# One 512-column matmul for the high weights in place of two of 256, with a split accumulator

## The chip, the cores and the metric

The kernel runs on one core of a Trainium2 chip. The metric is the device time of one execution in microseconds (us); less is better. The engines are called PE (TensorE, matmuls; PEld is its weight load), DVE (VectorE), ACT (ScalarE), POOL (GpSimd) and SP (which here only starts transfers). TensorE's granted clock is 0.992 of full speed as a mean over the profiled span.

## The reference

A trunk of two decoder layers over 256 positions, model width 2048. Every sub-layer computes h = RMSNorm(x) * (1 + scale) + shift, and then x += gate * f(h), where shift, scale and gate are linear in SiLU(c) (one vector c of 2048, weights `ada_w`).

- Layer 0: one input projection (`ab_w_in`), latent attention and a gated DeltaNet on its columns, one output projection (`ab_w_out`).
- Layer 1: gated linear attention ("GLA", `gla_w_in`, `gla_w_out`).
- After each: a SwiGLU feed-forward network ("FFN"), `(silu(h @ w1) * (h @ w3)) @ w2`, with 5632 inner columns. The two are called FFN 0 and FFN 1.
- At the end one RMSNorm.

All inputs and the output are float32.

## The kernel before

**Matmuls in parts.** A weight tile arrives as float32 (`raw`). ACT rounds it to float32r (`hi`, L255) and DVE subtracts (`lo = raw - hi`, L256, which the profile shows as L195). Activations are split in the same way into two halves of one tile, `hl[:, 0]` (high) and `hl[:, 1]` (low), 256 tokens each. `mm3` (L263) then makes a product of three matmuls: hi x high, hi x low and lo x high, each with a stationary weight tile of 128 x 128, 256 moving columns, and the same [128, 256] PSUM accumulator. Below, such three matmuls are a *triple*: one k-tile (128 rows of the weights) of one block (128 output columns).

**Streaming.** `stream_T` (L269) computes 512 output columns at a time: a *group* of four blocks with one PSUM bank each (`acc`, a pool of four banks in all, L141). A weight load (`wload`, 512 rows x 512 columns, 1 MB) serves 16 triples: four blocks of four k-tiles. There are four `hi` and four `lo` buffers of two k-tiles each, so the load for the second wload ahead can be split only when PE lets go of a buffer. A group's block is emptied after its last k-tile by `evac`, and the next group's block of the same number needs that bank.

**Who empties what.** In the FFN `evac1` (L1267: ACT, SiLU), `evac3` (L1272: DVE product, then the split for the next product), and `x_add` (L472: DVE, x += gate * acc) after `w2`. `x_add` also follows the two output projections; the first of these is cut into three parts over k (k-tiles 0 to 7, 8 to 11, 12 to 15), so each of its 16 blocks is added three times. The GLA projections copy their accumulators out (L1330, L1346).

**Order.** A scheduler places each engine's instructions in advance; each engine then runs its own list in order. In between, DVE makes `ada` sums (L202, `ada<-araw,sc,ada`: 128 x 512 multiply-adds of `ada_w`) at a rate tied to the weight loads, until they are all done, in layer 1's GLA; FFN 1 has none. In FFN 0 these keep their program order.

Of the kernel before, what the change touches and what calls it, by code (L numbers as in the profile page):

```python
# [26 lines left out]


def _constants():
# [20 lines left out]
    # out[m] = sum_k lhsT[k, m] x[k]  # L50
# [32 lines left out]
def weave(main, back, n_back=1, rest=True):  # L83
    """Emit `main`, with `n_back` steps of `back` after each of its steps; then the rest of `back`."""
    due = 0.0
    for _ in main:
        due += n_back
        while due >= 1 - 1e-9:
            due -= 1
            if next(back, StopIteration) is StopIteration:  # L90
                due = -1e9
    if rest:
        drain(back)


def braid(*gens):
    """The generators' steps in turn."""
# [34 lines left out]
class Trunk:  # L132
# [74 lines left out]
    def lnexp(s):  # L207
        """Load the table set that has both logarithm and exponential."""
        s.tc.keep_in_program_order(s.nc.scalar.preload_act_table_set("natural_log_exp_and_others"))

    def tick(s, n):
        """n steps of the background stream."""
# [10 lines left out]
    def split(s, hl, x):  # L223
        """hl [128, 2, n] float32r: the high and the low part of x [128, n], which sum to x."""
# [3 lines left out]
    def rstd(s, out, ss, n, eps=EPS):  # L228
        """out = (ss / n + eps) ** -0.5, from logarithm and exponential with a Newton step."""
# [17 lines left out]
    def wload(s, src, k0, nk, c0, ncol, tick=False):  # L247
        """Per k-tile, the high and low parts of src's columns, [128, ncol] each."""
# [14 lines left out]
    def mm3(s, ps, w, hl, start, stop):  # L263
        """ps += w^T h: w (hi, lo) stationary, hl [128, 2, T] moving."""
# [3 lines left out]

    def stream_T(s, src, k0, hs, c0, ncol, evac, nk=None, prepare=None):  # L269
        """Blocks of (h @ src[k0.., c0:c0+ncol])^T; evac(block, psum [128, T])."""  # L270
# [3 lines left out]
        for t in range(0, nk, 4):  # L274
# [6 lines left out]
            for b in range(nb):  # L281
                for q in range(n):
                    w = tuple(x[:, b * 128:(b + 1) * 128] for x in ws[q])
                    s.mm3(ps[b][:, :T], w, hs[t + q], t + q == 0, t + q == nk - 1)
                if t + n == nk:
                    evac(b, ps[b][:, :T])
                yield

    def stream_few(s, src, k0, hs, c0, ncol, evac):
        """As stream_T, two blocks to a bank; evac(pair of blocks, psum [128, 2 T])."""  # L290
# [15 lines left out]
    def stream_narrow(s, pieces, k0, hs, out, start, stop):  # L306
        """At most four k-tiles of 80 columns: those of `pieces` [(src, c0, n)], then zeros; out psum [80, T]."""
# [18 lines left out]
    def ada_all(s, jobs, ahead=None, wide=False):  # L326
        """silu(c) @ ada_w[l, m] + ada_b for each job (l, m, cols, pe), `cols` being groups of four column tiles
        or [(first, number)], four at most; on the tensor engine or on the vector engine; the loads run ahead."""
# [32 lines left out]
    def ada_ends(s):  # L361
        """What is due of the ends of units."""
# [6 lines left out]
    def ada_flush(s):  # L369
        """All ends of the units that are done."""  # L370
# [48 lines left out]
    def ada_rows(s):  # L419
        """The sums over the partitions of the units in s.fin, in rows; ada_end is to follow."""  # L420
# [11 lines left out]
    def ada_end(s, a, us, sel):  # L432
        """Rows, 32 to a unit (or the one unit), to columns; with bias, and scale 1 + s times the norm's."""
# [38 lines left out]
    def x_add(s, l, m, k, ps):  # L472
        s.stt(s.x[:, k], ps, s.gate(l, m, k), s.x[:, k], ALU.mult, ALU.add)

    def x_square(s, k):
        """The square of x's k-tile, into the sum over them; of the last ones straight in the product with ones."""
# [34 lines left out]
    def setup(s):  # L511
# [36 lines left out]
        # 1 / rms of the tokens, then along the free axis  # L548
# [45 lines left out]
    def rope_tables(s):  # L594
        """cos and signed sin of positions * inv_freq, [128, T]; exact reduction for any int32 position."""
# [12 lines left out]
        n = s.d((128, 2, T))      # n1, n0  # L608
        r = s.d((128, 2, T))      # remainder, parts
        w = s.d((128, 2, T))  # L610
        # ang = n1 2^22 + n0 2^12 + a2
# [7 lines left out]
        # k = round((n1 b22 + n0 b12 + a2) / 2 pi)  # L619
# [6 lines left out]
        # coarse parts, on a grid of 2^-11, are exact  # L626
# [12 lines left out]
        # cos x = sin(x + pi/2), wrapped  # L639
# [9 lines left out]
    def in_proj(s):  # L649
# [24 lines left out]
        for c, nk in enumerate(chunks):  # L674
# [7 lines left out]
            for name, g, c0 in order:  # L682
# [30 lines left out]
                def evac1(b, ps):  # L713
                    f = P[name, 2 * g + b // 2][:, b % 2]
                    s.tt(f, ps, f, ALU.add)
# [19 lines left out]
    def conv(s, which, blk, out):  # L735
        """out = silu(causal depthwise convolution of block blk)."""
# [9 lines left out]
    def gdn(s):  # L746
# [37 lines left out]
        # natural layout: logarithms of the squared norms, decay and beta  # L784
# [8 lines left out]
        lnss = s.pers((128, 2, 2, 8), name="lnss")      # tile, (k, q), head  # L793
# [19 lines left out]
        bg = s.sv((128, 2, 16))       # ln beta, g  # L813
# [42 lines left out]
    def gdn_local(s, half):  # L856
        """Per head: the decayed products of keys and queries, and the natural layouts."""
# [4 lines left out]
        # L^T of the half's heads and chunks, with room to read it in steps of a block row and a block  # L862
        s.lt[half] = s.drp.tile([8, 8 * 2064], F32, name=s.nm("lt"))
        for hh in range(4 * half, 4 * half + 4):
# [30 lines left out]
            nt = s.d((128, 4, 128))       # beta v (both chunks), k for the state, k for w  # L895
# [7 lines left out]
    def gdn_blocks(s, half):  # L903
        """(I + L)^-1 of the blocks of 16 on the diagonal, and its transpose, by substitution, a block a partition;
        then as [128, (T, R), unit, 16], rows on partitions."""
# [8 lines left out]
        for _ in range(W0):       # steps of the others, while the blocks are on their way  # L914
# [18 lines left out]
    def gdn_merge(s, half):  # L933
        """R = (I + L)^-T from its blocks of 16. T = R^T and R are kept as their blocks of 32, [128, unit, 32],
# [700 lines left out]
```

## Time and profile before

| | |
|---|---|
| Median of 3 runs | 2667.74 us (2664.41 to 2672.6) |
| Profiled execution, span from first to last instruction | 2669.5 us |
| PE busy | 2635.0 us, 99% |
| PEld busy | 2448.4 us, 92% |
| DVE busy | 1752.1 us, 66% |
| ACT busy | 1158.9 us, 43% |
| DMA moved | 622.73 MB, 233 GB/s |

No time of the profiled execution is listed apart from its span; the span lies within the range of the timed runs, 1.8 us above their median. Busy time of PE counts pipelined matmuls that overlap, so the pace of matmuls is read from the distance of their starts, not from their durations.

### The profile page before, as it was taken

The page shows a single profiled execution, that of the slowest core. Times are in us where ns is not written, and L with a number is a line of the kernel's source. Part 1 is how long each engine was busy: PE and PEld are TensorE (multiplying, and loading weights), DVE is VectorE, ACT ScalarE, POOL GpSimd, SP SyncE. Part 2 cuts the span into 40 slices and gives each one's busy share as a digit, 9 for nine tenths or more (in the row PEclk, how much of TensorE's full clock was granted, in tenths as well). Part 3 has the DMA queues.
Part 4 walks back from the last instruction along what each step waited for, and adds up shares of the span by engine and source line. Part 5 has one row for each costly group of instructions (what it writes and reads, how often), then busy time and mean ns, then how long its engine had stood idle before and what let it go on. Part 6 is the DMA issues. An engine that isn't in the chain of part 4 may idle for free.

```text
span 2669.5 us, 49809 instructions
## 1 busy us (share of the span) xinstructions
PE 2635.0 (99%) x20850; PEld 2448.4 (92%) x20850; DVE 1752.1 (66%) x2566; ACT 1158.9 (43%) x1705; POOL 108.2 (4%) x166
## 2 busy tenths in 40 slices
PE   8999999999999999999999999999999999999998
PEld 5778886788999999999999998999999999999998
DVE  3655763678888878878889687775554544544544
ACT  4324574534433344333335444564444344333334
POOL 0000004002000000000002000002000000000001
PEclk9999999999999999999999999999999999999999
DMA  9886654787898889888896655545455555555553
GB/s 332 294 273 219 211 196 157 246 281 242 298 337 304 309 302 323 299 306 315 301 321 223 219 185 199 190 155 187 160 179 189 177 187 182 181 189 176 188 180 120
DMA packets 324111, 622.73 MB, mean 233 GB/s; under 512 B 20192, under 2 KB 31085, under 8 KB 323887
## 3 DMA queue, kind: packets, MB, share of 16 engines
q1 hardware_dynamic: 319998, 606.76, 66.6%
q0 software_dynamic: 3696, 12.72, 1.4%
q8 instruction: 163, 2.67, 0.4%
q14 instruction: 62, 0.50, 0.1%
q10 hardware_dynamic: 192, 0.08, 0.0%
HBM read 616.09 MB, written 3.41 MB: 232 GB/s over the span
## 4 chain that ended last, share of the span: by engine, by line
PE 97%; DMA 1%; DVE 1%; ACT 0%; issue 0%; SPq 0%; DVEq 0%; ACTq 0%
PE acc L192 87%; PE sm L192 6%; PE pa L192 4%; DMA araw<-in_ada_w 1%; DMA d<-in_ada_w 0%; ACT hi L255 0%; DVE lo L195 0%; DMA d<-in_x 0%; ACT d L205 0%; DVE tmp L195 0%; PE acc L1503 0%; DVE tmp L202 0%; PE acc L1218 0%; PE acc L893 0%; PE acc L894 0%
## 5 line engine op out<-in xcount | busy, mean ns | idle before, releaser
L192 PE MATMUL acc<-d,hi 128*128 128x256 f32 x12000 | 2193.7, 285 | 10.7 <-ACT d L205 10.4
L192 PEld LDWEIGHTS acc<-d,hi 128*128 128x128 f32 x12000 | 1876.2, 192 | 82.5 <-issue 35.7
L192 PE MATMUL acc<-d,lo 128*128 128x256 f32 x6000 | 1696.2, 284 | 0.0
L195 DVE TENSOR_TENSOR lo<-raw,hi 128x1024 fp32r<-128x1024 f32 (+2 forms) x801 | 946.5, 1204 | 615.8 <-ACT hi L255 592.3
L255 ACT CAST hi<-raw 128x1024 fp32r<-128x1024 f32 x776 | 781.7, 1045 | 1076.2 <-PE acc L192 932.0
L192 PEld LDWEIGHTS acc<-d,lo 128*128 128x128 f32 x6000 | 1150.2, 192 | 15.7 <-issue 13.8
L202 DVE SCALAR_TENSOR_TENSOR ada<-araw,sc,ada 128x512 f32<-128x512 f32 x480 | 362.7, 757 | 5.3
L202 DVE SCALAR_TENSOR_TENSOR x<-acc,mod,x 128x256 f32<-128x256 f32 x192 | 89.6, 480 | 61.9 <-PE acc L192 61.9
L195 DVE TENSOR_TENSOR d<-acc,d 128x256 f32<-128x256 f32 (+1 forms) x168 | 80.4, 486 | 71.9 <-PE acc L192 70.6
L192 PE MATMUL pa<-araw,sc 128*32 128x512 f32 x480 | 119.3, 611 | 5.4 <-DMA araw<-in_ada_w 5.3
L192 PE MATMUL acc<-hi,d 128*128 128x512 f32 (+1 forms) x320 | 93.4, 373 | 0.0
L225 ACT CAST d<-d 128x256 fp32r<-128x256 f32 x128 | 47.7, 404 | 49.7 <-DVE d L195 49.7
L192 PEld LDWEIGHTS acc<-hi,d 128*128 128x128 f32 x320 | 57.8, 189 | 10.6 <-ACT tmp L1203 0.8
L195 DVE TENSOR_TENSOR d<-d,d 128x256 fp32r<-128x256 f32 (+1 forms) x155 | 60.9, 421 | 8.9 <-ACT d L205 5.2
L205 ACT ACTIVATE d<-acc 128x256 f32<-128x256 f32 x96 | 36.7, 383 | 56.7 <-PE acc L192 56.7
L192 PE MATMUL acc<-lo,d 128*128 128x512 f32 (+1 forms) x160 | 59.9, 374 | 0.0
L195 POOL TENSOR_TENSOR ss<-ss,tmp 128x256 f32<-128x256 f32 x44 | 52.8, 1199 | 79.2 <-ACT tmp L205 77.5
L195 DVE TENSOR_TENSOR tmp<-d,tmp 128x512 f32<-128x512 f32 x64 | 43.7, 689 | 2.3 <-ACT tmp L205 1.9
L481 POOL COPY ss<-tmp 128x256 f32<-128x256 f32 x3 | 1.3, 421 | 964.3 <-ACT tmp L205 964.3
L205 ACT ACTIVATE d<-tmp,mod 128x256 fp32r<-128x256 f32 x64 | 28.6, 501 | 26.9 <-DVE tmp L202 14.2
L192 PEld LDWEIGHTS pa<-araw,sc 128*32 128x32 f32 x480 | 17.0, 107 | 24.7 <-DMA araw<-in_ada_w 8.2
L205 ACT ACT_TABLE_LOAD x28 | 35.9, 1283 | 3.5 <-DVE d L1350 1.4
(214 smaller groups left out, 1083.2 us busy)
## 6 DMA issues: line engine op xcount, KB each, us to landing
raw<-in_ffn_w SPq DMA_DIRECT2D x264, 1024.0 KB, 5.2
araw<-in_ada_w SPq DMA_DIRECT2D x347, 512.0 KB, 6.0
raw<-in_gla_w_in SPq DMA_DIRECT2D x48, 1024.0 KB, 5.1
raw<-in_ab_w_in SPq DMA_DIRECT2D x30, 1024.0 KB, 6.0
raw<-in_ab_w_out SPq DMA_DIRECT2D x16, 1024.0 KB, 6.9
raw<-in_gla_w_out SPq DMA_DIRECT2D x16, 1024.0 KB, 5.0
araw<-in_ada_w POOLq DMA_DIRECT2D x21, 512.0 KB, 4.2
raw<-in_ab_w_in SPq DMA_DIRECT2D x20, 512.0 KB, 5.9
```

Source lines behind the costliest of these rows:

```text
L192: s.nc.tensor.matmul(out, lhsT=lhsT, rhs=rhs, start=start, stop=stop)
L195: (eng or s.nc.vector).tensor_tensor(out=out, in0=a, in1=b, op=op)
L202: return s.nc.vector.scalar_tensor_tensor(out=out, in0=a, scalar=sc, in1=b, op0=op0, op1=op1)
L205: s.nc.scalar.activation(out, a, f, **kw)
L225: s.nc.scalar.copy(hl[:, 0], x)
L255: s.nc.scalar.copy(hi[:, :n, :ncol], raw[:, a:a + n, :ncol])
L481: s.nc.gpsimd.tensor_copy(s.ss, q)
```

## The change

The high weights multiply both halves of the activations in one matmul of 512 columns, whose output fills the whole bank: hi x high in the left 256 columns, hi x low in the right 256. The product lo x high goes to the left half. Per k-tile there are two matmuls where there were three, with the same 768 moving columns. After a block's first k-tile, lo stands ahead of hi. Whoever empties a bank adds its halves: `join` copies the right half with ACT and adds the left with DVE; `x_add` and `evac1` of the input projection make two DVE instructions of one. The other users of `mm3` keep it.

```diff
+    def mmw(s, ps, w, hl, first, last):
+        both = hl.rearrange("p a t -> p (a t)")
+        if first:
+            s.mm(ps, w[0], both, True, False)
+            s.mm(ps[:, :T], w[1], hl[:, 0], False, False)
+        else:
+            s.mm(ps[:, :T], w[1], hl[:, 0], False, False)
+            s.mm(ps, w[0], both, False, last)
+
+    def join(s, out, ps):
+        s.nc.scalar.copy(out, ps[:, T:])
+        s.tt(out, ps[:, :T], out, ALU.add)
...
-                    s.mm3(ps[b][:, :T], w, hs[t + q], t + q == 0, t + q == nk - 1)
+                    s.mmw(ps[b], w, hs[t + q], t + q == 0, t + q == nk - 1)
                 if t + n == nk:
-                    evac(b, ps[b][:, :T])
+                    evac(b, ps[b])
...
     def x_add(s, l, m, k, ps):
-        s.stt(s.x[:, k], ps, s.gate(l, m, k), s.x[:, k], ALU.mult, ALU.add)
+        for a in range(2):
+            s.stt(s.x[:, k], ps[:, a * T:(a + 1) * T], s.gate(l, m, k), s.x[:, k], ALU.mult, ALU.add)
...
                 def evac1(b, ps):
                     f = P[name, 2 * g + b // 2][:, b % 2]
-                    s.tt(f, ps, f, ALU.add)
+                    for a in range(2):
+                        s.tt(f, ps[:, a * T:(a + 1) * T], f, ALU.add)
...
-                    s.act(sl[b // 2][:, b % 2], ps, AF.Silu)
+                    a = sl[b // 2][:, b % 2]
+                    s.join(a, ps)
+                    s.act(a, a, AF.Silu)
...
                     t = sl[b // 2][:, b % 2]
-                    s.tt(t, ps, t, ALU.mult)
+                    u = s.tmp((128, T))
+                    s.join(u, ps)
+                    s.tt(t, u, t, ALU.mult)
...
-                    if nme == "q":
-                        s.act(dst[key][:, b % 2], ps, AF.Copy, scale=1.0 / 16.0)
-                    else:
-                        nc.vector.tensor_copy(dst[key][:, b % 2], ps)
+                    o = dst[key][:, b % 2]
+                    s.join(o, ps)
+                    if nme == "q":
+                        s.act(o, o, AF.Copy, scale=1.0 / 16.0)
...
-                (nc.scalar.copy if b % 2 else nc.vector.tensor_copy)(s.gr[key][:, b % 2], ps)
+                s.join(s.gr[key][:, b % 2], ps)
```

The scheduler makes new lists from this. First PE, at the end of one `w2` group of FFN 0 and the start of the next (in the kernel before, the end of the group of acc1557 to acc1560, a block's four k-tiles in a row; `hi1569` holds k-tiles 0 and 1 of a wload, `hi1572` k-tiles 2 and 3):

```order
L192 MATMUL acc1558_9289<-d1415_8134,hi1569_9357 128x256 x2
L192 MATMUL acc1558_9289<-d1415_8134,lo1570_9358 128x256
L192 MATMUL acc1558_9289<-d1416_8150,hi1569_9357 128x256 x2
L192 MATMUL acc1558_9289<-d1416_8150,lo1570_9358 128x256
L192 MATMUL acc1558_9289<-d1417_8166,hi1572_9365 128x256 x2
L192 MATMUL acc1558_9289<-d1417_8166,lo1573_9366 128x256
L192 MATMUL acc1558_9289<-d1418_8182,hi1572_9365 128x256 x2
L192 MATMUL acc1558_9289<-d1418_8182,lo1573_9366 128x256
L192 MATMUL acc1559_9290<-d1415_8134,hi1569_9357 128x256 x2
```

The same engine in the changed kernel, the very end of the group acc1573 to acc1576 (`hi1594` holds the last two of its 12 k-tiles) and the first rows of the next group, whose block 0 is acc1597:

```order
L192 MATMUL acc1573_8368<-d1500_7921,hi1594_8475 128x512
L192 MATMUL acc1574_8369<-d1498_7906,lo1595_8476 128x256
L192 MATMUL acc1574_8369<-d1498_7906,hi1594_8475 128x512
L192 MATMUL acc1574_8369<-d1500_7921,lo1595_8476 128x256
L192 MATMUL acc1574_8369<-d1500_7921,hi1594_8475 128x512
L192 MATMUL acc1575_8370<-d1498_7906,lo1595_8476 128x256
L192 MATMUL acc1575_8370<-d1498_7906,hi1594_8475 128x512
L192 MATMUL acc1575_8370<-d1500_7921,lo1595_8476 128x256
L192 MATMUL acc1575_8370<-d1500_7921,hi1594_8475 128x512
L192 MATMUL acc1576_8371<-d1498_7906,lo1595_8476 128x256
...
L192 MATMUL acc1576_8371<-d1500_7921,hi1594_8475 128x512
L192 MATMUL acc1597_8523<-d1349_6998,hi1602_8529 128x512
```

Two matmuls stand for three, and the blocks now take turns every two k-tiles: block 0 (acc1573) ends only three pairs of k-tiles before the group does, and the next group's block 0 follows at once.

Next DVE, which empties such a group in FFN 0. In the kernel before (group acc1557 to acc1560):

```order
L202 SCALAR_TENSOR_TENSOR x19_117<-acc1557_9288,mod16_114,x19_117 128x256
L202 SCALAR_TENSOR_TENSOR ada1567_9304<-araw1571_9361,sc11_104,ada1567_9304 128x512
L202 SCALAR_TENSOR_TENSOR x19_117<-acc1558_9289,mod16_114,x19_117 128x256
L202 SCALAR_TENSOR_TENSOR x19_117<-acc1559_9290,mod16_114,x19_117 128x256
L202 SCALAR_TENSOR_TENSOR ada1567_9304<-araw1574_9369,sc11_104,ada1567_9304 128x512
L202 SCALAR_TENSOR_TENSOR x19_117<-acc1560_9291,mod16_114,x19_117 128x256
L195 TENSOR_TENSOR lo1594_9560<-raw1592_9557,hi1593_9559 128x1024
```

In the changed kernel (group acc1573 to acc1576):

```order
L202 SCALAR_TENSOR_TENSOR x19_117<-acc1573_8368,mod16_114,x19_117 128x256
L195 TENSOR_TENSOR lo1610_8580<-raw1608_8577,hi1609_8579 128x1024
L202 SCALAR_TENSOR_TENSOR x19_117<-acc1574_8369,mod16_114,x19_117 128x256
L202 SCALAR_TENSOR_TENSOR x19_117<-acc1575_8370,mod16_114,x19_117 128x256
L202 SCALAR_TENSOR_TENSOR ada1583_8384<-araw1590_8433,sc11_104,ada1583_8384 128x512
L202 SCALAR_TENSOR_TENSOR x19_117<-acc1573_8368,mod16_114,x19_117 128x256
L202 SCALAR_TENSOR_TENSOR x19_117<-acc1576_8371,mod16_114,x19_117 128x256
L195 TENSOR_TENSOR lo1612_8584<-raw1608_8577,hi1611_8583 128x1024
L202 SCALAR_TENSOR_TENSOR x19_117<-acc1574_8369,mod16_114,x19_117 128x256
L202 SCALAR_TENSOR_TENSOR x19_117<-acc1575_8370,mod16_114,x19_117 128x256
L202 SCALAR_TENSOR_TENSOR ada1583_8384<-araw1590_8433,sc11_104,ada1583_8384 128x512
L202 SCALAR_TENSOR_TENSOR x19_117<-acc1576_8371,mod16_114,x19_117 128x256
```

A block's bank was free after one instruction; now the second half of block 0 is read after four others. In FFN 1, where no `ada` sums are left, only one `lo` stands between the two halves of block 0:

```order
L202 SCALAR_TENSOR_TENSOR x19_117<-acc3672_21052,mod16_114,x19_117 128x256
L195 TENSOR_TENSOR lo3702_21239<-raw3700_21236,hi3701_21238 128x1024
L202 SCALAR_TENSOR_TENSOR x19_117<-acc3672_21052,mod16_114,x19_117 128x256
L202 SCALAR_TENSOR_TENSOR x19_117<-acc3673_21053,mod16_114,x19_117 128x256
L202 SCALAR_TENSOR_TENSOR x19_117<-acc3674_21054,mod16_114,x19_117 128x256
```

The first `x` row and the third are the two halves of one block; before, there was one row for it.

## Rows read from the trace of the kernel before

**Rows 1.** The page: span, busy time of engines, and the chain that ended last.
```profile
span 2669.5 us, 49809 instructions
...
PE 2635.0 (99%) x20850; PEld 2448.4 (92%) x20850; DVE 1752.1 (66%) x2566; ACT 1158.9 (43%) x1705; POOL 108.2 (4%) x166
...
PE 97%; DMA 1%; DVE 1%; ACT 0%; issue 0%; SPq 0%; DVEq 0%; ACTq 0%
```

**Rows 2.** Timeline of FFN 1: start, length (us), engine, line, operation, tiles, count.
```profile
2000.24 0.40 PE L192 MATMUL acc<-d,hi 128*128 128x256 f32 x2
2000.37 0.19 PEld L192 LDWEIGHTS acc<-d,lo 128*128 128x128 f32 x1
2000.48 0.28 PE L192 MATMUL acc<-d,lo 128*128 128x256 f32 x1
2000.48 0.31 PEld L192 LDWEIGHTS acc<-d,hi 128*128 128x128 f32 x2
2000.60 0.40 PE L192 MATMUL acc<-d,hi 128*128 128x256 f32 x2
```

**Rows 3.** Timeline of PE in GLA's values, matmuls of 512 columns.
```profile
1639.95 0.61 PE L192 MATMUL acc<-hi,d 128*128 128x512 f32 x2
1640.40 0.39 PE L192 MATMUL acc<-lo,d 128*128 128x512 f32 x1
1640.63 0.61 PE L192 MATMUL acc<-hi,d 128*128 128x512 f32 x2
```

**Rows 4.** Lines by form, PE: count | busy us, mean ns | idle before, releasers.
```profile
L192 PE MATMUL acc<-d,hi 128*128 128x256 f32 x11936 | 2182.5, 285 | 10.7 <-ACT d L205 10.4 <-DVE d L195 0.2
L192 PE MATMUL acc<-d,lo 128*128 128x256 f32 x5968 | 1687.3, 284 | 0.0
```

**Rows 5.** Windows: stretch, length, busy us of PE, PEld, DVE, ACT, POOL, clock, DMA share, GB/s.
```profile
600.00:700.00 100.00, 96.02 (x730) 87.87 (x730) 84.01 (x139) 46.26 (x74) 15.61 (x12) 0.97 0.72 243
...
1000.00:1100.00 100.00, 100.00 (x825) 98.06 (x824) 81.75 (x114) 38.71 (x47) 0.00 (x0) 1.00 0.89 311
...
2100.00:2200.00 100.00, 100.00 (x836) 100.00 (x835) 48.05 (x54) 37.66 (x43) 0.00 (x0) 1.00 0.56 184
```

**Rows 6.** Lines by form, DVE, 700 to 1400 us (FFN 0).
```profile
L195 DVE TENSOR_TENSOR lo<-raw,hi 128x1024 fp32r<-128x1024 f32 x234 | 282.3, 1221 | 110.4 <-ACT hi L255 110.3
L202 DVE SCALAR_TENSOR_TENSOR ada<-araw,sc,ada 128x512 f32<-128x512 f32 x338 | 252.0, 748 | 4.3
L202 DVE SCALAR_TENSOR_TENSOR x<-acc,mod,x 128x256 f32<-128x256 f32 x48 | 22.5, 480 | 4.4 <-PE acc L192 4.4
L195 DVE TENSOR_TENSOR d<-acc,d 128x256 f32<-128x256 f32 x43 | 17.9, 421 | 3.8 <-PE acc L192 3.8
...
L199 DVE TENSOR_SCALAR ada<-araw,sc 128x512 f32<-128x512 f32 x23 | 11.0, 480 | 1.8 <-DMA araw<-in_ada_w 1.8
```

**Rows 7.** Timeline of DVE in FFN 0 (paces of its operations).
```profile
1016.27 0.42 DVE L195 TENSOR_TENSOR d<-acc,d 128x256 f32<-128x256 f32 x1
1016.60 0.42 DVE L195 TENSOR_TENSOR d<-d,d 128x256 fp32r<-128x256 f32 x1
1016.94 0.75 DVE L202 SCALAR_TENSOR_TENSOR ada<-araw,sc,ada 128x512 f32<-128x512 f32 x1
1017.60 0.42 DVE L195 TENSOR_TENSOR d<-acc,d 128x256 f32<-128x256 f32 x1
...
1044.74 2.32 DVE L202 SCALAR_TENSOR_TENSOR ada<-araw,sc,ada 128x512 f32<-128x512 f32 x3
1047.56 2.36 DVE L195 TENSOR_TENSOR lo<-raw,hi 128x1024 fp32r<-128x1024 f32 x2 [0.51 <-ACT hi L255]
```

**Rows 8.** Timeline of DVE in FFN 1, end of a w2 group.
```profile
2303.57 0.48 DVE L202 SCALAR_TENSOR_TENSOR x<-acc,mod,x 128x256 f32<-128x256 f32 x1 [0.96 <-PE acc L192]
2303.97 2.35 DVE L195 TENSOR_TENSOR lo<-raw,hi 128x1024 fp32r<-128x1024 f32 x2
2309.56 2.36 DVE L195 TENSOR_TENSOR lo<-raw,hi 128x1024 fp32r<-128x1024 f32 x2 [3.25 <-ACT hi L255]
```

**Rows 9.** Windows of 30 us at the end of layer 0's output projection, columns as in rows 5.
```profile
590.00:620.00 30.00, 30.00 (x204) 22.07 (x201) 21.25 (x37) 10.37 (x16) 0.00 (x0) 1.00 0.88 299
620.00:650.00 30.00, 30.00 (x250) 29.10 (x248) 28.91 (x46) 14.71 (x26) 15.61 (x12) 1.00 0.79 259
```

**Rows 10.** The chain in order of time, its last long piece: start, us, what.
```profile
1891.75 763.14 PE acc L192 x6336
```

## The prediction, made before the result was known

> **What bounds the kernel now.** I read the page first. PE is busy 99% of the span, its weight loads 92%, DVE 66%, and the chain that ended last is 97% PE [rows 1]. So time is won by what makes PE's list shorter, and lost by what lets PE wait. Busy time of PE doesn't say how fast it goes, since a matmul's row of 0.28 us overlaps the next; the timeline does. In FFN 1 the first hi matmul of a triple starts at 2000.24 us and the next triple's at 2000.60: 0.360 us for three matmuls of 256 columns, 0.120 each [rows 2]. 256 columns at 2.4 GHz (the granted clock in FFN 1 is 1.00 of it [rows 5]) are 106.7 ns, so each matmul costs 13.3 ns beside its columns. The kernel has matmuls of 512 columns too, in GLA's values: a round of three takes from 1639.95 to 1640.63, 0.680 us, so 226.7 ns each [rows 3]. 512 columns are 213.3 ns; the rest is 13.3 ns again. So there is a fixed price per matmul, whatever its width, and it is the same with hi and lo weights.
>
> Then I looked at who keeps PE fed. In FFN 1 DVE is busy 48 of 100 us, in FFN 0 81.75 of 100, and at the end of layer 0's output projection 28.91 of 30 [rows 5, 9]. FFN 0 is where DVE's list could become as long as PE's, because it carries the `ada` sums there as well [rows 6].
>
> **What the change takes away.** Two matmuls of 256 become one of 512: 2 x 120.0 - 226.7 = 13.3 ns per triple, 346.7 instead of 360.0. Rows 4 count 5968 triples (11936 hi, 5968 lo). From the code, 400 of them stay as they are (320 in the input projection's early chunks, 80 in the latent attention). The other 5568: 2112 in each FFN (11 groups x 4 blocks x 16 k-tiles for w1, the same for w3, 16 blocks x 44 for w2), 256 in each output projection, 512 in GLA's q, k and r, 320 in the input projection's last chunk. 5568 x 13.3 ns = 74.2 us, of which 28.2 in each FFN, 6.8 in GLA's input, 3.4 in each output projection, 4.3 in the input projection. It lies wholly on the chain. The weight loads stay hidden: they have rows of 0.19 us but follow each other at 0.12 now, and a 512-column matmul gives more room for the next.
>
> At the first place the Trainium skill is against this. TensorE: Matmul & The Clock Gate, in "Wait — 56ns, not 53.3ns?", gives a fixed cost of about 2.5 ns for a warm matmul, on top of its columns; by that figure the sum would be an estimated 5568 x 2.5 = 14 us, less than what is given back below. The trace disagrees: 13.3 ns at both widths [rows 2, 3], and the measurement decides.
>
> **What it adds, and where that is hidden.** Every emptied block costs DVE one more instruction, and most cost ACT one more copy. Paces on DVE, from start to start: an `x` add 0.40 us (2303.57 to 2303.97) [rows 8], an add out of PSUM 0.33 (1016.27 to 1016.60), a `lo` about 1.13, from two rows in 2.36, an `ada` 0.66 before another operation and 0.78 in a row of three, so 0.72 [rows 7]. `ada` steps per wload in FFN 0: 361 in 117 wloads (234 `lo` rows), 3.1, of which 23 are shorter [rows 6]; I use 3.
>
> *FFN 1* (no `ada`). A w2 group of three wloads takes PE 16.64 us; DVE 6 x 1.13 + 8 x 0.40 = 10.0. The question is the bank. In the new order the last k-tiles are done two at a time over the four blocks, so block 0 ends 3 x 0.69 = 2.08 us before the group, and the next group wants its bank at once. DVE needs `x`, `lo`, `x` = 0.40 + 1.13 + 0.40 = 1.93 us. Just hidden; I allow 0.2 us at each of 16 group ends, 3 us (0 to 8). w1 and w3 groups have 4 to 6 us for a bank, and a copy, an add and a `lo` in between need less.
>
> *FFN 0, w2.* The same end of group, but with `x`, `lo`, `x`, `x`, `ada`, `x` = 1.60 + 1.13 + 0.66 = 3.4 us against 2.08: PE waits 1.3 us. Going through the order of all 16 groups I find 12 with such a path longer than its cover, by 0.6 to 2.6 us, some 18 us together. Beside that DVE's work for such a group, 6 x 1.13 + 8 x 0.40 + 9 x 0.72 = 16.5 us, is 99% of PE's 16.64. Bounds: 0 if DVE's rows run ahead of PE's and the waits vanish, 18 + 16 x 1.13 = 36 us if DVE also comes one `lo` late at each.
>
> *FFN 0, w1 and w3.* A w3 group takes PE 22.19 us now (23.04 before); DVE has 8 `lo` (9.04), 12 `ada` (8.64) and 12 adds and products (4.0 where it was 2.7): 21.7 us, 98%. w1: 9.04 + 8.64 + 1.3 = 19.0, 86%. So w3 is at the edge and w1 gives back. I take 0.5 us for each of 11 w3 groups, 5 us (0 to 15).
>
> *Layer 0's output projection.* 48 more `x` adds x 0.40 = 19.2 us on a DVE that is 96% busy in the last 30 us but 71% in the 30 before [rows 9]. The scheduler has moved 21 of 34 `ada` steps of this stretch ahead of it (14 us), into earlier room. I take 8 us (0 to 19).
>
> *The rest.* GLA's input and the second output projection have some 50 small instructions more on a DVE with room: 2 us (0 to 10). At the ends of five stages the last block's extra instruction (0.4 us, and a hand-over) is bare: 3 us (2 to 5). The input projection, attention and DeltaNet are laid out anew by the scheduler around stalls that are there already: 3 us (-10 to 15).
>
> Sum: -74.2 + 3 + 18 + 5 + 8 + 2 + 3 + 3 = -32 us. The profiled span of 2669.5 us becomes 2637. The median of the runs is 1.8 us below the span, less than a quarter of the runs' own spread, and I leave that out: I predict **2637 us**.
>
> **Rivals.**
>
> *The whole saving.* The scheduler's order has rivals of its own for DVE, and a stall at a group's end gives DVE time that it would lack later. If only the bare ends cost (3 us) and FFN 0 and the output projection hide theirs as they do now (PE sat idle for 10.7 us in all ahead of hi matmuls, and not at all ahead of lo [rows 4]), the time is 2669.5 - 74 + 5 = 2600. For it: DVE's work is under 100% everywhere. Against: three places over 95%.
>
> *FFN 0 gives nothing.* If the group ends and w3 cost twice what I take (46 us), and the output projection 12, the rest as above (11): -74 + 69 = -5, 2664. For it: the same places; against: FFN 1's 25 us stand on a DVE that is half idle.
>
> *Slower: DVE bounds FFN 0.* DVE's list is run in order, and it waits for ACT's `hi` 110.4 us in 700, that is 0.94 us per wload [rows 6]. If these waits stay where they are while the work grows, a wload takes DVE 16.5/3 + 0.94 = 6.4 us in w2, 21.7/4 + 0.94 = 6.4 in w3 and 5.7 in w1, where PE takes 5.55. Then FFN 0's 132 wloads cost 88 x 0.85 + 44 x 0.15 = 81 us above PE's pace. With 8 + 11 elsewhere: -74 + 100 = +26, 2696. It decides as soon as such waits exceed 5.55 - 5.50 = 0.05 us per wload in w2 and 5.55 - 5.43 = 0.12 in w3. Against it: a wait for `hi` is what is left when DVE is early, since PE frees the buffer; a late DVE doesn't have it. In the output projection, where DVE is 96% busy, PE still goes on.
>
> *The change doesn't do what it says.* If a lo matmul behind a 512-column one took 133 ns, the triple would stay at 360 and only the cost remain: +42, 2712. No row shows the mixed sequence; both pure ones have the same fixed part, which speaks against it.
>
> **How the numbers follow.** About my sum (2618 to 2655): 0.60. Nearly the whole saving (2595 to 2618): 0.16. Mostly eaten (2655 to 2676): 0.13, half of it within 0.3% of 2667.7 (8 us: what can be told from no change). Slower, by DVE in FFN 0: 0.08; no shorter triple: 0.03. The range leaves out the last two and the outermost part of the others: 2598 to 2668. Faster by over 0.3% 0.82, within 0.3% 0.07, slower 0.11.
>
> **What would show it.** Triples start every 0.347 us in FFN 1, which shrinks from 763 us of unbroken PE [rows 10] by 25 to 28. PE rows fall by 5568. In FFN 0 the windows show DVE over 90% and PE gaps of 1 to 2 us at w2 group ends, with an `x` row as what ended them, and none inside w1 groups. In the output projection `x` adds take twice the time. If FFN 0 is longer than its 760 us before, the third rival is right; if there are no gaps at its w2 ends, the first. If the triple is not 0.347, the first term is wrong and with it everything.

## The result, and the profile after

The changed kernel takes 2684.04 us (median of 5 runs, 2676.66 to 2685.4); the kernel before takes 2666.65 us on the same chip. The ratio is 1.0052, 95% interval 1.0036 to 1.0069: slower by 17 us, where 2637 was forecast. The page of the changed kernel, the lines that answer to [rows 1] and [rows 4]:

```profile
span 2679.8 us, 39138 instructions
...
PE 2600.2 (97%) x15282; PEld 2153.7 (80%) x15282; DVE 1895.7 (71%) x2990; ACT 1231.3 (46%) x1905; POOL 102.5 (4%) x166
...
PE 89%; DVE 6%; ACT 2%; issue 2%; DMA 1%; POOL 0%; SPq 0%; DVEq 0%; ACTq 0%; POOLq 0%
...
L192 PE MATMUL acc<-d,hi 128*128 128x512 f32 (+1 forms) x6432 | 2121.2, 385 | 45.4 <-DVE x L202 22.5
```

PE has exactly 5568 instructions fewer. But DVE now holds 6% of the chain (1% before), and PE stood idle 45.4 us ahead of hi matmuls (10.7 before), half of it for an `x` add.

**By stage.** A stage begins where DVE computes the 1/rms of the tokens (`rs`). Timeline of DVE, these rows, before and after:

```profile
654.80 0.43 DVE L202 SCALAR_TENSOR_TENSOR rs<-tmp,tmp 128x256 f32<-128x256 f32 x1
1453.75 0.42 DVE L202 SCALAR_TENSOR_TENSOR rs<-tmp,tmp 128x256 f32<-128x256 f32 x1
1890.11 0.42 DVE L202 SCALAR_TENSOR_TENSOR rs<-tmp,tmp 128x256 f32<-128x256 f32 x1
```

```profile
657.99 0.42 DVE L202 SCALAR_TENSOR_TENSOR rs<-tmp,tmp 128x256 f32<-128x256 f32 x1
1487.54 0.42 DVE L202 SCALAR_TENSOR_TENSOR rs<-tmp,tmp 128x256 f32<-128x256 f32 x1
1917.94 0.42 DVE L202 SCALAR_TENSOR_TENSOR rs<-tmp,tmp 128x256 f32<-128x256 f32 x1
```

| stage | before | after | difference | forecast |
|---|---|---|---|---|
| to layer 0's output projection | 654.8 | 658.0 | +3 | +3 |
| FFN 0 | 798.9 | 829.6 | **+31** | -4 |
| GLA and its projections | 436.4 | 430.4 | -6 | -8 |
| FFN 1 | 779.4 | 761.8 | -18 | -24 |

(The forecast's terms are sorted by stage, with one of the 3 us of stage ends in each FFN.) The differences are those of the two profiled executions, whose spans are 10 us apart where the medians are 17. FFN 0 alone makes 35 of the 43 us by which the span of 2679.8 us is above the forecast. The distances between the starts of successive matmuls, all of FFN 0 taken together, say what it consists of, in us (the last distance is counted whole, also where it runs over the stage's end; so the columns add up to 798.1 and 832.2):

| FFN 0 | before | after |
|---|---|---|
| its matmuls at 120.0 and 226.7 ns | 760.3 | 732.2 |
| each somewhat later than that | 4.7 | 17.9 |
| under the halved clock | 2.0 | 9.0 |
| over 0.2 us late | 0 | 20.4 |
| distances behind other matmuls (`ada` rows, stage ends) | 31.1 | 52.7 |

**Waits at the ends of w2 groups.** PE, then DVE, at one such end in FFN 0 of the changed kernel (in brackets: idle before, releaser):

```profile
874.46 0.40 PE L192 MATMUL acc<-d,hi 128*128 128x512 f32 x1
877.05 0.48 PE L192 MATMUL acc<-d,hi 128*128 128x512 f32 x1 [2.19 <-DVE x L202]
```

```profile
873.45 0.48 DVE L202 SCALAR_TENSOR_TENSOR x<-acc,mod,x 128x256 f32<-128x256 f32 x1
873.85 1.21 DVE L195 TENSOR_TENSOR lo<-raw,hi 128x1024 fp32r<-128x1024 f32 x1
874.98 0.87 DVE L202 SCALAR_TENSOR_TENSOR x<-acc,mod,x 128x256 f32<-128x256 f32 x2
875.76 0.74 DVE L202 SCALAR_TENSOR_TENSOR ada<-araw,sc,ada 128x512 f32<-128x512 f32 x1
876.42 0.87 DVE L202 SCALAR_TENSOR_TENSOR x<-acc,mod,x 128x256 f32<-128x256 f32 x2
```

This is the order x, lo, x, x, ada, x that the prediction priced at 3.4 us: 873.45 to 876.9. The group ends at 874.7; the next waits 2.19 us for an `x`.

**The clock.** At another such end PE waits 2.33 us, and then goes at half the clock. PE's timeline there, and the windows of two such places (columns as in [rows 5]):

```profile
1155.62 0.54 PE L192 MATMUL acc<-d,hi 128*128 128x512 f32 x1 [2.33 <-DVE x L202]
...
1157.45 0.41 PE L192 MATMUL acc<-d,lo 128*128 128x256 f32 x1
1157.67 0.63 PE L192 MATMUL acc<-d,hi 128*128 128x512 f32 x1
1158.09 0.42 PE L192 MATMUL acc<-d,lo 128*128 128x256 f32 x1
```

```profile
1155.90:1159.30 3.40, 3.40 (x12) 2.93 (x11) 3.37 (x7) 0.00 (x0) 0.00 (x0) 0.50 0.88 294
1336.80:1343.60 6.80, 6.12 (x20) 5.28 (x21) 6.42 (x11) 0.00 (x0) 0.00 (x0) 0.50 0.92 321
```

A triple takes 0.64 us there (1157.45 to 1158.09) instead of 0.353: 0.50 is the level of 1.2 GHz. Three of FFN 0's interior waits, of 2.33, 2.67 and 2.77 us, went with such a fall. Before there was none inside FFN 0, where PE is never idle; the window of the kernel before from 700 to 1450 us:

```profile
700.00:1450.00 750.00, 750.00 (x6117) 731.44 (x6116) 615.00 (x810) 290.05 (x358) 14.64 (x12) 1.00 0.88 312
```

**The pace.** In the stretch 1000 to 1100 us, in FFN 0, PE waits for nothing: its lines by form there (count | busy us, mean ns | idle before), and then the windows that answer to [rows 5, 9]:

```profile
L192 PE MATMUL acc<-d,hi 128*128 128x512 f32 x272 | 94.7, 398 | 0.0
L192 PE MATMUL acc<-d,lo 128*128 128x256 f32 x272 | 73.1, 282 | 0.0
L192 PE MATMUL sm<-ada,cst 128*32 128x512 f32 x6 | 3.1, 604 | 0.0
L192 PE MATMUL sm<-cst,tmp 128*128 128x4 f32 x8 | 0.9, 242 | 0.0
```

```profile
590.00:620.00 30.00, 28.65 (x173) 24.74 (x171) 29.78 (x59) 13.60 (x22) 0.00 (x0) 1.00 0.47 158
620.00:650.00 30.00, 24.36 (x112) 20.06 (x113) 29.11 (x55) 10.86 (x20) 9.58 (x10) 0.83 0.64 211
...
1000.00:1100.00 100.00, 100.00 (x558) 84.44 (x557) 87.45 (x133) 44.43 (x66) 0.00 (x0) 1.00 0.88 308
...
2100.00:2200.00 100.00, 99.54 (x567) 86.08 (x566) 57.98 (x79) 40.62 (x49) 0.00 (x0) 1.00 0.56 189
```

FFN 0: 272 triples in some 96 us (100 less the 14 small matmuls), 0.353 us each. FFN 1: 567 instructions in 99.5 us, 0.351, with four starts among them that come 0.28 us late; without these delays 0.349. Forecast was 0.347. From hi to lo it is 233 ns on average in FFN 1, from lo to hi 116: the 512 columns cost 6 ns more than in GLA's values [rows 3], the 256 columns 4 less than before.

### The profile page after: what moved, and what is told of

Same layout as the page of the kernel before. It is cut to its first block, busy times and chain, and to the rows that moved or that the text cites. A ratio compares the mean times of both kernels' runs of the same rounds, so it can differ in the third digit from the quotient of the medians.

```text
span 2679.8 us, 39138 instructions
## 1 busy us (share of the span) xinstructions
PE 2600.2 (97%) x15282; PEld 2153.7 (80%) x15282; DVE 1895.7 (71%) x2990; ACT 1231.3 (46%) x1905; POOL 102.5 (4%) x166
## 4 chain that ended last, share of the span: by engine, by line
PE 89%; DVE 6%; ACT 2%; issue 2%; DMA 1%; POOL 0%; SPq 0%; DVEq 0%; ACTq 0%; POOLq 0%
PE acc L192 79%; PE sm L192 6%; PE pa L192 4%; DVE lo L195 2%; DVE x L202 1%; DVE ada L202 1%; ACT hi L255 1%; ACT L205 0%; DMA raw<-in_ffn_w 0%; DVE tmp L202 0%; DVE d L195 0%; DMA d<-in_x 0%; ACT d L205 0%; DVE tmp L195 0%; PE sm L562 0%
## 5 line engine op out<-in xcount | busy, mean ns | idle before, releaser
L192 PE MATMUL acc<-d,hi 128*128 128x512 f32 (+1 forms) x6432 | 2121.2, 385 | 45.4 <-DVE x L202 22.5
L192 PE MATMUL acc<-d,lo 128*128 128x256 f32 x6000 | 1619.9, 283 | 4.2 <-ACT d L205 1.7
L192 PEld LDWEIGHTS acc<-d,hi 128*128 128x128 f32 x6432 | 1162.9, 190 | 312.6 <-issue 73.6
L202 DVE SCALAR_TENSOR_TENSOR x<-acc,mod,x 128x256 f32<-128x256 f32 x384 | 167.7, 476 | 23.8 <-PE acc L192 22.6
L195 DVE TENSOR_TENSOR d<-acc,d 128x256 f32<-128x256 f32 (+1 forms) x240 | 107.4, 464 | 86.2 <-PE acc L192 63.3
L192 PE MATMUL pa<-araw,sc 128*32 128x512 f32 x480 | 106.5, 607 | 2.7 <-DMA araw<-in_ada_w 2.6
L205 ACT ACTIVATE d<-d 128x256 f32<-128x256 f32 (+1 forms) x138 | 62.9, 466 | 21.8 <-DVE d L202 10.0
L282 ACT COPY d<-acc 128x256 f32<-128x256 f32 x120 | 43.9, 369 | 44.4 <-PE acc L192 42.9
L282 ACT COPY tmp<-acc 128x256 f32<-128x256 f32 x88 | 32.5, 369 | 39.0 <-PE acc L192 39.0
L205 ACT ACTIVATE tmp<-x 128x256 f32<-128x256 f32 x64 | 25.3, 411 | 37.2 <-DVE x L202 37.2
```

What stands on the lines that cost most here:

```text
L192: s.nc.tensor.matmul(out, lhsT=lhsT, rhs=rhs, start=start, stop=stop)
L195: (eng or s.nc.vector).tensor_tensor(out=out, in0=a, in1=b, op=op)
L202: return s.nc.vector.scalar_tensor_tensor(out=out, in0=a, scalar=sc, in1=b, op0=op0, op1=op1)
L205: s.nc.scalar.activation(out, a, f, **kw)
L282: s.nc.scalar.copy(out, ps[:, T:])
```

## The experiments

Times are medians; the ratio to the kernel before (2666.6 to 2669.3 us in the four sets of runs) stands with its interval. The stages of each profiled run, in us, in the order of the first table; stage 0 is all that stands before FFN 0 (a stage of unchanged code varies by up to 6 us in the first and 1 to 4 in the others; the profiled run of e7_ada took 2689.5 us, the longest of its six):

| kernel | us | ratio, interval | stage 0 | FFN 0 | GLA | FFN 1 |
|---|---|---|---|---|---|---|
| before | 2666.7 | | 654.8 | 798.9 | 436.4 | 779.4 |
| after | 2684.0 | 1.0052, 1.0036 to 1.0069 | 658.0 | 829.6 | 430.4 | 761.8 |
| e1_layer1 | 2646.8 | 0.9926, 0.9913 to 0.9938 | 652.5 | 798.4 | 430.1 | 762.7 |
| e2_ffn0 | 2707.8 | 1.0150, 1.0135 to 1.0165 | 652.3 | 832.3 | 439.8 | 779.2 |
| e3_split | 2707.2 | 1.0150, 1.0136 to 1.0164 | 656.6 | 833.4 | 436.7 | 778.7 |
| e4_left | 2642.3 | 0.9906, 0.9890 to 0.9921 | 656.6 | 792.4 | 429.4 | 758.7 |
| e5_pool | 2710.8 | 1.0161, 1.0141 to 1.0181 | 683.0 | 813.6 | 437.6 | 769.2 |
| e6_w13 | 2646.4 | 0.9923, 0.9911 to 0.9936 | 653.9 | 799.9 | 430.1 | 763.0 |
| e7_ada | 2679.5 | 1.0046, 1.0030 to 1.0062 | 663.2 | 831.8 | 430.8 | 762.0 |
| e8_acc5 | 2673.7 | 1.0028, 1.0013 to 1.0043 | 666.9 | 798.7 | 439.8 | 764.4 |
| e10_act | 2683.1 | 1.0056, 1.0040 to 1.0072 | 671.7 | 808.9 | 436.1 | 761.3 |
| e11_reduce | 2683.1 | 1.0050, 1.0033 to 1.0067 | 682.8 | 805.6 | 434.7 | 758.3 |
| e12_l1red | 2645.5 | 0.9915, 0.9899 to 0.9930 | 650.6 | 799.1 | 434.6 | 758.8 |
| e13_f0red | 2676.2 | 1.0027, 1.0017 to 1.0037 | 653.8 | 804.6 | 436.1 | 780.1 |
| e14_dma | 2659.0 | 0.9965, 0.9952 to 0.9977 | 650.8 | 799.3 | 432.9 | 771.1 |
| e15_best | 2646.9 | 0.9913, 0.9899 to 0.9928 | 656.4 | 799.7 | 430.9 | 759.0 |

### Where the loss sits: layer 1 alone, FFN 0 alone

`stream_T` and each emptying function choose by stage between the old and the new form (the edits further down are shown against this version):

```diff
-                    s.mmw(ps[b], w, hs[t + q], t + q == 0, t + q == nk - 1)
+                    if wd:
+                        s.mmw(ps[b], w, hs[t + q], t + q == 0, t + q == nk - 1)
+                    else:
+                        s.mm3(ps[b][:, :T], w, hs[t + q], t + q == 0, t + q == nk - 1)
```

> Only layer 1 (GLA's q, k and r, its output projection, FFN 1) has the merged matmul; layer 0 is as in the kernel before. Theory A (the loss sits in layer 0, where DVE is full and comes late to the accumulators at group ends): layer 0 as before, layer 1 shorter by the 6.0 + 17.6 us read from the two traces, so about 2643 (2638 to 2650). Rival B (the stages are tied together: what FFN 1 won in the changed kernel was work done earlier in the longer layer 0, or the merged form itself gains nothing): within 8 us of before, 2659 to 2675.

> Only FFN 0 (w1, w3, w2) has the merged matmul; all else is as before. Theory A: FFN 0 alone makes its 31 us of loss, about 2697 (2688 to 2706), with PE gaps of 1 to 3 us at the ends of w2 groups. Rival B (FFN 0 is only longer because it inherits work that the input projection and the output projection put off): 2655 to 2675, and few gaps.

2646.8 is theory A; 2707.8 is 2 us above its range, far from the rival's. The stages are nearly independent: -21 and +40 add to +19, the whole change gives +17, so layer 0's projections are worth about -2, which is less than the runs' own spread.

### Emptying without the gain, and the gain with half the x adds

```diff
...
-            s.mm(ps, w[0], both, False, last)
+            s.mm(ps[:, :T], w[0], hl[:, 0], False, False)
+            s.mm(ps[:, T:], w[0], hl[:, 1], False, last)
```

```diff
-        for a in range(2 if wd else 1):
+        for a in range(1):
             s.stt(s.x[:, k], ps[:, a * T:(a + 1) * T], s.gate(l, m, k), s.x[:, k], ALU.mult, ALU.add)
```

> The accumulator is split and emptied exactly as in the changed kernel, but three matmuls of 256 columns fill it, so nothing is won on PE. Theory A (the emptying costs, the merged matmul gains some 11 ns a triple in FFN 1 and 5 in FFN 0, about 42 us in all): 2684 + 42 = 2726 (2712 to 2735). Rival B (the sequence of 512 and 256 columns is what stalls PE, the emptying is hidden as forecast): 2667 to 2690, and no gaps at w2 group ends in FFN 0.

> As the changed kernel, but an x add reads the left half alone, as one instruction (the products of hi weights and lo activations of w2 and of both output projections are left out of the sum). Theory A (the doubled x adds are the path at the ends of w2 groups): the gaps of FFN 0 go, with the clock falls behind them, about 2648 (2638 to 2660). Rival A2 (DVE's whole work, ada and lo, and not the path at the group end is what is late): still 2672 to 2684.

The emptying alone costs 40 us (2707.2, 5 us below theory A's range and far above rival B's), of which 35 in FFN 0. The merged matmul gives back 23 of them, not the 42 that theory A expected: in FFN 0 it gives 4, and waits over 0.2 us are 20.4 us there where the split form has 15.1, so part of a faster PE's gain goes into longer waits. Without the second x adds the time is 2642.3, 42 us less (theory A); FFN 0 is 37 us shorter, and between 700 and 1400 us no wait of PE is left in its trace. So the second x adds are the cause of the loss. Whether by DVE's time or by the way to the bank, this run doesn't say.

### DVE's time, or the way to the bank?

```diff
+            if s.skip and k % 5 in (1, 3):
+                return
             a = u["a"][:, :w]
```

```diff
-        s.accp = ctx.enter_context(tc.tile_pool(name="accp", bufs=4, space=PSUM))
-        s.smp = ctx.enter_context(tc.tile_pool(name="smp", bufs=3, space=PSUM))
+        s.accp = ctx.enter_context(tc.tile_pool(name="accp", bufs=5, space=PSUM))
+        s.smp = ctx.enter_context(tc.tile_pool(name="smp", bufs=2, space=PSUM))
```

```diff
-            s.stt(s.x[:, k], ps[:, a * T:(a + 1) * T], s.gate(l, m, k), s.x[:, k], ALU.mult, ALU.add)
+            u = s.tmp((128, T))
+            s.nc.vector.tensor_reduce(out=u, in_=ps.rearrange("p (a t) -> p t a", a=2), axis=AX.X, op=ALU.add)
+            s.stt(s.x[:, k], u, s.gate(l, m, k), s.x[:, k], ALU.mult, ALU.add)
```

> As the changed kernel, but two of five steps of the ada sums that run on DVE in FFN 0 are left out (part of the modulation is then missing): 0.4 x 361 x 0.72 = 104 us of DVE, as much as the second x adds of FFN 0 (256 x 0.40 = 102), but spread over all groups. Rival A2 (DVE's whole work is the bound): as e4_left in FFN 0, 2645 to 2655. Theory A (the instructions that stand between a block and its bank at the group's end): the w2 gaps mostly stay, 2662 to 2678.

> As the changed kernel, with five accumulator banks and two for the small products (4 and 3 before). Theory A (PE waits at the group's end because block 0's bank is not free): a fifth bank covers the first block, w2 gaps shrink, 2650 to 2668. Rival A2 (DVE is late as a whole, so any spare bank is used up): 2675 to 2690.

> As the changed kernel, but DVE empties a block of w2 or of an output projection with one instruction, a reduction over the two halves into SBUF, and adds that times the gate to x afterwards. DVE gets more to do (a pass over 512 columns is 0.66 us by the ada rows, and the add 0.40: 1.06 against 0.80 us per block, 0.26 x 256 = 67 us in FFN 0), but the bank hangs on one instruction. Theory A (the way to the bank decides): 2640 to 2665, faster than the changed kernel although DVE has more work. Rival A2 (DVE's time decides): 2690 to 2740.

FFN 0 from 700 to 1400 us, windows of the changed kernel, of e7_ada and of e11_reduce (sum of PE, PEld, DVE, ACT, POOL):

```profile
700.00:1400.00 700.00, 681.52 (x3739) 571.97 (x3738) 591.49 (x854) 286.20 (x388) 0.00 (x0) 0.99 0.87 303
```

```profile
700.00:1400.00 700.00, 682.54 (x3753) 572.63 (x3753) 502.69 (x725) 288.63 (x392) 0.00 (x0) 0.99 0.85 301
```

```profile
700.00:1400.00 700.00, 697.69 (x3866) 586.51 (x3864) 621.41 (x887) 301.46 (x412) 0.00 (x0) 1.00 0.89 311
```

Waits of PE (in all, times, longest), the changed kernel from 700 to 1430 us and e7_ada from 700 to 1435:

```profile
PE acc L192 <- DVE x L202: 16.1, 8, 2.8
```

```profile
PE acc L194 <- DVE x L204: 15.2, 11, 2.1
```

With 89 us less work on DVE (72% busy instead of 84%) PE waits as long for `x` adds as before. With 30 us more (89% busy), but one instruction between a block and its bank, PE does 127 instructions more, and from 725 to 1430 us no wait of PE is listed. That settles it for FFN 0: the way to the bank, not DVE's time. The fifth bank agrees: FFN 0 is 31 us shorter and has one wait of 1.3 us from 700 to 1405 us. (e7_ada's time, 2679.5, is 2 us above A's range, 24 above A2's.) By its whole time e8_acc5 (2673.7; its twelve runs lie between 2668 and 2684) lies between both expectations: stage 0 and the GLA stage became 9 us longer each. These have many small products, which now have two banks; that this is the reason isn't shown by a run of its own.

The whole time of e11_reduce (2683.1) fits neither expectation. What FFN 0 gained, the stage before lost: PE waits for reductions between 540 and 683 us:

```profile
PE acc L193 <- DVE tmp L495: 14.4, 10, 4.2
```

In two of the output projection's three passes a group is one wload of four k-tiles, 16 x 0.35 = 5.6 us for PE; DVE needs 2 x 1.13 + 4 x (0.60 + 0.40) = 6.3 for it with the reduction (0.60 from start to start in its trace) and 5.5 with two adds. There DVE's sum is the bound. That is worked out, and no run of its own shows it.

### Other ways to empty

```diff
-        for a in range(2 if wd else 1):
-            s.stt(s.x[:, k], ps[:, a * T:(a + 1) * T], s.gate(l, m, k), s.x[:, k], ALU.mult, ALU.add)
+        s.act(u, ps[:, T:], AF.Copy, scale=s.gate(l, m, k))
+        s.stt(s.x[:, k], ps[:, :T], s.gate(l, m, k), s.x[:, k], ALU.mult, ALU.add)
+        s.tt(s.x[:, k], s.x[:, k], u, ALU.add, s.nc.gpsimd)
```

e10_act has DVE in the last line, behind the left half.

> As the changed kernel, but an x add is one DVE instruction again: ACT copies the right half times the gate out of the bank, DVE adds the left half times the gate, and GpSimd adds the copy to x. Theory A (two DVE adds per block are what comes late): as with the left half alone, 2642 plus a little, 2636 to 2652. Rival B (GpSimd's adds slow DVE, or the longer path to the bank through ACT stalls PE as much): 2658 to 2685.

> As the changed kernel, with as many DVE instructions, but only one of an x add reads the bank: DVE adds the left half times the gate, ACT copies the right half times the gate into SBUF, and DVE adds the copy to x later. Theory A (PE waits for what stands between a block's last matmul and its bank): the w2 gaps of FFN 0 shrink as far as ACT comes in time behind its casts of 1.05 us, 2650 to 2670. Rival A2 (DVE's whole work): unchanged, 2678 to 2690. Rival B (ACT's place in the path costs as much, as with GpSimd in e5_pool): 2690 to 2715.

e5_pool (2710.8) is slower than even rival B allowed: FFN 0 is 16 us shorter than in the changed kernel, but stage 0 is 25 longer and the GLA stage and FFN 1 are 7 longer each. A GpSimd add takes 0.97 us, and what squares x waits for it. e10_act (2683.1) is in A2's range, but not for A2's reason: FFN 0 is 21 us shorter, stage 0 14 longer, GLA 6 longer.

### FFN 0 by itself, with the short way

> Layer 1 merged as in e1_layer1, and of layer 0 only FFN 0's w1 and w3; w2, both of layer 0's projections as before. Theory A (the loss is the doubled x adds): 1408 triples gain 5 to 8 ns each, so 2647 - 9 = 2638 (2632 to 2644). Rival A2 (DVE's whole work decides, w3 groups at 98% of PE): 2650 to 2662, with gaps inside w3 groups.

> FFN 0 alone merged, as in e2_ffn0 (2707.8 us), with the reduction in place of the two x adds of w2. Theory A (e2's loss is the wait for the bank at w2 group ends, with the clock that falls behind it): 27 to 37 us less than e2_ffn0, 2671 to 2681; what is then left above the kernel before is pace and stage ends. Rival A2 (DVE's time, of which the reduction takes 17 us more): 2707 or slower. A gain on the kernel before (under 2660) would mean that only the x adds spoilt FFN 0.

2646.4 for e6_w13: the merged form in w1 and w3 of FFN 0 gives nothing over e1_layer1; A was off by 2, and A2 by 4. e13_f0red is theory A: 2676.2, 32 us less than e2_ffn0 through the one instruction. Still it is slower than before. Its FFN 0 by the table above: 732.2 + 16.9 (pace) + 2.6 (clock) + 8.3 (late) + 43.1 (behind other matmuls), against 760.3 + 4.7 + 2.0 + 0 + 31.1. Of the 28 us won 12 go to the pace, 15 to the stage's first 35 and last 55 us, where all of the remaining waits stand, and 6 to distances behind `ada` rows in between, without a wait: more than was won.

### The pace, and the best version

```diff
+        s.owed += s.extra
+        while s.owed >= 1:
...
+            r = s.arp.tile([128, 2, 512], F32, tag="araw", name=s.nm("araw"))
+            s.nc.sync.dma_start(r, s.h["ada_w"][0, 0][256 * s.turn:256 * s.turn + 256, 0:512].rearrange(
...
```

> As e15_best, but in FFN 1 each wload also brings 1.5 loads of 512 KB that nobody reads, the traffic that the ada loads make in FFN 0. Theory D (the DMA traffic slows the mixed sequence of matmuls): its 2112 triples go from 0.350 to 0.353 us or more, FFN 1 becomes 6 to 12 us longer than in e15_best. Rival: the pace stays, within 3 us of e15_best.

> Layer 1 alone merged, as in e1_layer1, with the reduction in place of the two x adds. Theory A: the 14 short gaps of FFN 1 in e1_layer1 (4.8 us) go, 2647 - 4 = 2643 (2639 to 2647). Rival (they are not waits for the bank, or the longer instruction makes new ones): 2646 to 2655.

> Layer 1 alone merged; two x adds in its output projection (stage of 430.1 us in e1_layer1), the reduction in FFN 1 (758.8 us in e12_l1red). Theory A adds up the stages: 652 + 799 + 430 + 759 = 2640 (2637 to 2644). Rival (the 434.6 us of the stage in e12_l1red had another cause): 2644 to 2648.

FFN 1 from 2150 to 2250 us, windows of e15_best and of e14_dma; and e14_dma's waits of PE from 2000 to 2600:

```profile
2150.00:2250.00 100.00, 100.00 (x575) 87.29 (x575) 55.07 (x72) 48.54 (x75) 0.00 (x0) 1.00 0.59 189
```

```profile
2150.00:2250.00 100.00, 100.00 (x569) 86.87 (x568) 55.29 (x68) 46.64 (x67) 0.00 (x0) 1.00 1.01 384
```

```profile
PE acc L194 <- DVE lo L197: 3.6, 9, 0.5
```

Theory D holds in part. In this stretch, with twice the traffic, 569 matmuls fit where 575 did, 0.3515 us a triple instead of 0.3478. Over FFN 1 as a whole, where the mean traffic was 291 GB/s against 189, the distances add up to 4.6 us more. The stage became 12 us longer; the rest is mostly starts that wait for `lo`, whose weights land later (6.1 us from issue to landing, median of all `ffn_w` loads, against 5.5).

But the slower pace doesn't need more traffic. FFN 1 of e8_acc5, with five accumulator banks, is as slow at 187 GB/s and without a wait: by the count of the FFN 0 table its pace is 12.3 us above 732.2, the changed kernel's 5.4. Windows from 1950 to 2600 us of e15_best, e14_dma and e8_acc5:

```profile
1950.00:2600.00 650.00, 649.66 (x3717) 566.24 (x3716) 382.88 (x493) 289.87 (x395) 0.40 (x1) 1.00 0.58 189
```

```profile
1950.00:2600.00 650.00, 645.85 (x3659) 558.63 (x3659) 377.98 (x483) 287.65 (x389) 0.00 (x0) 1.00 0.81 291
```

```profile
1950.00:2600.00 650.00, 650.00 (x3688) 564.75 (x3687) 370.16 (x488) 286.37 (x391) 0.00 (x0) 1.00 0.57 187
```

And the mixed sequence doesn't have one pace but two. First and last rows of two stretches of e15_best's FFN 1, of five triples and of six, with no wait in them:

```profile
2200.34 0.27 PE L193 MATMUL acc<-d,lo 128*128 128x256 f32 x1
...
2202.07 0.28 PE L193 MATMUL acc<-d,lo 128*128 128x256 f32 x1
```

```profile
2150.05 0.28 PE L193 MATMUL acc<-d,lo 128*128 128x256 f32 x1
...
2152.16 0.28 PE L193 MATMUL acc<-d,lo 128*128 128x256 f32 x1
```

That is 0.346 us a triple, the value forecast, and 0.352. The starts in the trace, in ns, show two patterns that repeat: 231, 112, 233, 117 for two triples (346.5 each), and 117, 241, 120, 236, 113, 233 for three (353.3 each). A stage's pace is the mix of both. Distances from one lo to the next of over 351 ns, which of the two patterns only the slower one has, are 34% in e15_best's FFN 1, 51% in e14_dma's, 70% in e8_acc5's and 58% in the FFN 0 of e13_f0red. FFN 0 is 10.7 us behind FFN 1 in pace (16.9 in e13_f0red, 6.2 in e15_best). 4 us of that lie in the sequence itself, which runs more often in the slower pattern there. 6 us are some 70 single starts about 0.1 us late, most of them next to the small matmuls; the 4.7 us of the kernel before are of this kind. What makes PE take one pattern or the other stays open; the traffic may be a part of it, and isn't the only thing that can.

The Trainium skill says in SBUF — State Buffer, "SBUF: two separate sides", that the engines' ports and those of the DMA are apart and a DMA and a compute operation don't slow each other. e14_dma shows PE 1% slower under 384 GB/s, with no wait between its matmuls; the runs don't show through what.

e12_l1red took the short waits out of FFN 1 (762.7 to 758.8), as theory A said, but its GLA stage was longer; e15_best has 430.9 and 759.0 as A added up, but an untouched stage 0 that was 4 us longer than assumed, so that its time is in the rival's range. The medians of the three versions of layer 1 (2646.8, 2645.5, 2646.9) can't be told apart. Any of them beats both kernels, by 0.8% the one before and 1.4% the changed one.

## Why the prediction was wrong

The range failed on FFN 0: 4 us shorter were forecast, 31 longer measured. The mechanism of the group ends was right. What failed is the size of the first term, the size of the stage ends, and a term for the clock, which was missing.

**The first term, 74.2 us, was mis-sized.** The saving of 13.3 ns per triple rested on two pure sequences and the sentence "it lies wholly on the chain". The mixed sequence saves 11 ns in FFN 1 and 7 in FFN 0, which is 5 us less than forecast in the one and 13 less in the other: the forecast 346.7 ns is only the faster of its two patterns. The fourth rival pointed to this unknown, but only with all or nothing. The Trainium skill's 2.5 ns (TensorE: Matmul & The Clock Gate, "Wait — 56ns, not 53.3ns?") would put a triple at an estimated 320 + 5 = 325 ns; 346 to 353 were measured, so the trace still decides, but the pure sequences didn't carry over either.

**Group ends in FFN 0: mechanism right, size near.** 18 us (0 to 36) forecast; 16 of waits for `x` in the interior, eight of them, some 17 with what PE needs to start again. The `x` rows end them, as predicted. Beside them stand 3 us of other waits, and 6 us behind `ada` rows without a wait, for which there was no term. FFN 1's ends, 3 us (0 to 8) forecast, came to 3.4: twelve starts that are 0.28 us late.

**What followed from a wait was missing.** With three of the eight waits the clock went to half for 3 to 7 us. FFN 0 lost some 7 us to it; stage 0 also up to 7 (10.7 against 3.5 us by the same count, 3 of which are waits that fell into such a stretch; its window at 0.83). No term had it.

**Stage ends were mis-sized.** 3 us for five stages; FFN 0's two ends alone cost some 15 more than before. PE's timeline at its end, before and after:

```profile
1450.57 1.11 PE L192 MATMUL sm<-tmp,cst 128*128 128x256 f32 x4
1455.39 1.62 PE L192 MATMUL acc<-d,hi 128*128 128x256 f32 x5 [3.71 <-ACT d L205]
```

```profile
1479.31 0.70 PE L192 MATMUL sm<-tmp,cst 128*128 128x256 f32 x2 [1.55 <-ACT tmp L205]
1482.56 2.93 PE L192 MATMUL sm<-tmp,cst 128*128 128x256 f32 x6 [2.55 <-ACT tmp L205]
1490.33 0.76 PE L192 MATMUL acc<-d,hi 128*128 128x512 f32 x1 [4.84 <-DVE d L202]
```

The last blocks' second adds delay x, x's squares, their sum and the next stage's first tile, one behind the other: 4.84 + 2.55 + 1.55 us of waiting where it was 3.71. In e4_left, without these adds, the distances behind other matmuls in the stage's last 60 us come to 10 us where the changed kernel has 15 and the kernel before 9.

**Added up for FFN 0**, against the forecast: pace +13, stage ends +14, clock +7, `ada` rows +6, other waits +3, group ends -1, w3 -5. That is 37 us, where the stage's time is 35 above the forecast; the distances run over its end by some 3.

**w3 (5 us)** cost nothing that shows: no wait for a bank stands inside w1 or w3 groups, and e6_w13, where these alone are merged in FFN 0, has no wait of PE from 700 to 1400 us. **The output projection and the rest of stage 0 (+3) and the GLA stage** came out as forecast, though with waits and a lower clock that had no term there. For stage 0 that is in part luck: unchanged code varies by 6 us in it.

**The third rival had the place and the sign, not the cause.** "DVE bounds FFN 0" gave 2696, near to 2684. But DVE's sum decides nothing there: 15% of its work can go (e7_ada) and nothing changes, work can be added (e11_reduce) and the waits go; what changes the waits is the number of instructions between a block and its bank, or a spare bank (e8_acc5). The forecast had both views on the table, busy sum and group end, and gave this side 0.11 in all: it added up costs in FFN 0 against a saving that was taken as sure, although the whole of FFN 0's -4 us rested on it. The sign that it gave, a longer FFN 0, couldn't tell a full DVE from a late bank; the 760 us named there are FFN 0's matmuls alone, the stage took 798.9. DVE was 84% busy from 700 to 1400 us, and not over 90%.

**Slips in the working** that move little: the first rival names 3 us and adds 5, and four of the 16 `w2` groups have two wloads and not three.

## What to carry to other kernels

A saving per instruction is only sure in the sequence in which it will run: where no row shows the mixed sequence, give that its own bounds. When an accumulator is emptied by more instructions, count what stands between its last matmul and its release in the list of the emptying engine, not that engine's busy share; one longer instruction can beat two short ones, where the engine has the time (FFN 0), and can lose where its sum is the bound (the output projection, by the sum above). A stall of a few microseconds on TensorE can also cost the clock behind it (three of eight did here), so sum up stalls with what follows them, and apply the change only in the stages whose engines have room.

## What the runs showed that was not expected

- Matmuls of 512 and 256 columns in turn run in one of two patterns, 346.5 or 353.3 ns for the pair: 231 to 241 ns from hi to lo and 112 to 120 from lo to hi, where pure sequences take 227 and 120.
- 1% of PE's pace went with the DMA traffic (189 to 384 GB/s), without a wait in the trace; a fifth accumulator bank took about as much without more traffic.
- A wait of 2.33 us of PE was followed by 3.4 us at the level of 1.2 GHz in one place, and in another one of 2.37 us was not (the wait, and the window in which it ends, at 1.00):

```profile
1378.30 0.47 PE L192 MATMUL acc<-d,hi 128*128 128x512 f32 x1 [2.37 <-DVE x L202]
1378.00:1385.00 7.00, 6.70 (x37) 5.72 (x38) 6.93 (x13) 0.00 (x0) 0.00 (x0) 1.00 0.91 321
```
